# Layer 1 of a two-block transformer kernel in a pinned order with PSUM tiles, and 14 weight buffers in MLP 0

## The chip, the cores and the metric

The kernel runs on 1 core of one Trainium2 chip, in one launch. The metric is the device time of that core in microseconds (us); lower is better.

## The reference, cut to what matters

Sequence length 256, width 1024, float32 throughout. Two blocks follow each other; the change touches the first one, whose second layer is a gated linear recurrence.

```python
def mixer_c(h, w_in, conv_w, conv_b, w_r, b_r, w_i, b_i, lam, w_out):
    u = h @ w_in                                    # 1024 -> 2048
    gate, xr = jnp.split(u, 2, axis=-1)
    xr = causal_depthwise_conv(xr, conv_w) + conv_b # width 4
    y = rg_lru(xr, w_r, b_r, w_i, b_i, lam) * jax.nn.gelu(gate)
    return y @ w_out

def rg_lru(x, w_r, b_r, w_i, b_i, lam):             # 8 heads of 128
    r = sigmoid(einsum("bshi,hij->bshj", xb, w_r) + b_r)
    i = sigmoid(einsum("bshi,hij->bshj", xb, w_i) + b_i)
    log_a = -8.0 * r * softplus(-lam)
    a = exp(log_a); mult = sqrt(-expm1(2.0 * log_a))
    return scan(h_t = a_t * h_(t-1) + mult * i * x)

def first_block(x, ...):
    for layer in range(2):
        h = rmsnorm(x, mix_norm[layer])
        x = x + (mixer_ab(h, ...) if layer == 0 else mixer_c(h, ...))
        h = rmsnorm(x, mlp_norm[layer])
        x = x + square(relu(h @ w_up[layer])) @ w_down[layer]   # 1024 -> 4096 -> 1024
    return rmsnorm(x, final_norm)
```

The second block (latent attention and neighbourhood attention, with a modulation computed from a conditioning vector) follows; its arithmetic is untouched.

## The kernel before, in words

Activations lie transposed: 8 tiles of 128 channels by 256 positions. Every matrix product is made in three passes on TensorE (PE), high half times high half (L360), high times low (L361), low times high (L362), each a 128x128 weight against 256 columns. The host lays all weights out in the order of use, as 231 **units** of 128x1024 numbers (512 KB). One unit is 8 weights, so 24 products.

A unit takes this way: a DMA from SP's queue into one of RAW = 4 raw buffers (L300), a copy that makes the high half, on ACT (L307) or DVE (L309), and a subtraction that makes the low half, on DVE or POOL (L310). Which engines do it is set by `POLICY` for each name: "a" or "v" for the high half, "v" or "g" (POOL) for the low one. In layer 1 the names are `xr` (8 units, recurrence input), `ri` (2 units, the gates of four heads each), `cg` (8 units, the gelu branch) and `wo1` (8 units, the output product). `ready()` prepares the next unit of the plan; `unit(name)` takes one from the queue `self.q` and first prepares until `ahead` more stand behind it. Each `unit()` also runs one step of a background list, which in MLP 0 holds the modulation: 12 DMAs of 1 MB (`mw`) and 40 reductions on DVE (L883).

Prepared units lie in slots: RING = 6 (`wh`, `wl`) and, while the pool `wx` is open, EXTRA = 4 more (`wxh`, `wxl`). In MLP 0 `ahead` goes from 2 to FAR = 6 at pair 10 of 16:

```python
for p in range(16):
    if l == 0 and p == 10:
        self.ahead = FAR
    up(p)
```

The end of MLP 0 is `proj_tail` (L820 to L861): the last four units of `down` for all columns, in four column blocks, and after each block the residual sum on DVE (L835, L836), the high half of the next layer's input on ACT (L841, `xsh`), its low half on DVE (L847, `xsl`), a square on ACT (L855) and the running sum of squares on DVE (L857, `s`); at the end POOL folds the two halves of that sum (L861).

Layer 1 begins with `gfirst`, which interleaves the first two pairs of `xr` units by their depth: 6 of 8 steps of pair 0, 3 of pair 1, the rest of pair 0, the rest of pair 1. The norm comes in between: the column sums on PE (L424, `csum`), the variance on DVE (L430), its power -1/2 on POOL (L435, `rc`), and after both pairs the spread of it over the partitions on PE (L442) and ACT (L448, `R`). Each pair is then scaled by `R` (L1034), convolved over four taps by ACT (L1038) and DVE (L1042) into the SBUF tile `xc`, split into `xch` (ACT, L399) and `xcl` (DVE, L407) for each head, multiplied by the head's gate weights, passed through tanh (L1018, L1019, L1022) and exp (L1023), squared on DVE (L1026, L1027), rooted on ACT (L1057), scanned on DVE (L1064), multiplied by the gelu of the gate branch (L1048, L1050, L1066) and split for the output product (`xr`, `ysl`). Pair 3 of `xr` stands behind the first gate unit (RI0 = 6).

The order on each engine is set by a scheduler from priorities in program order and from dependences; `issue_after` adds a single edge.

Of the kernel before, what the change touches and what calls it, by code (L numbers as in the profile page):

```python
# [27 lines left out]
EXTRA = 4  # L28
FAR = 6
# [15 lines left out]
POLICY.update(val=("av", "ag", "av", "ag"), gate=("av", "av", "av", "ag"), xr=("av", "ag"), ri=("vg",), cg=("vg",))  # L45
# [24 lines left out]
def weight_plan(I):  # L70
# [48 lines left out]
    ri(1)  # L119
    for j in range(8):  # L120
        inn("cg", w, j * 128)
# [127 lines left out]
class Kern:  # L249
    def __init__(self, tc, aps, names, ctx):  # L250
        self.tc, self.nc, self.a, self.names, self.ctx = tc, tc.nc, aps, names, ctx
        self.n = 0
        self.u = 0
        self.raw = None
        self.bg = []
        self.q = []
        self.cnt = {}
        self.ahead = 2
        self.wx = None
        self.slot = 0  # L260

# [50 lines left out]
    def ready(self):  # L312
# [26 lines left out]
        self.q.append((name, (wh, wl)))  # L339

# [35 lines left out]
    def gfirst(self, name, x, mid=None):  # L376

        ps, ws = [self.ps(), self.ps()], [[], []]
        for a, k0, k1 in ((0, 0, GA), (1, 0, GB), (0, GA, 8), (1, GB, 8)):
# [7 lines left out]
            if k1 == 8 and mid:  # L387
                mid()
                mid = None
# [38 lines left out]
    def meaneps(self, ps, n, nt=2, tag="var"):  # L428
        v = self.t(self.cp, [128, nt], tag, bufs=2)
        self.nc.vector.tensor_scalar(v, ps, 1.0 / n, EPS, op0=ALU.mult, op1=ALU.add)  # L430
        return v
# [84 lines left out]
    def new_h(self, tag="xs"):  # L516
        return (self.t(self.cp, [128, 8, T], tag + "h", F32R), self.t(self.cp, [128, 8, T], tag + "l", F32R))
# [300 lines left out]
    def proj_tail(self, acc, name, ins, gname, g0, xs, R2=None, mp=None, sums=(), after=None):  # L818
# [4 lines left out]
        with self.tc.issue_after(after.ins) if after else nullcontext():  # L823
            ws = [self.unit(name) for _ in ins]
        n = len(ins)
        late = []
        for b in range(4):
# [17 lines left out]
            if xs is not None:  # L845
                for k in ks:
                    V.scalar_tensor_tensor(xs[1][:, k], x[:, k], g[k % 2], xs[0][:, k].bitcast(F32),  # L847
                                           op0=ALU.mult, op1=ALU.subtract)
            for i, (st, scaled) in enumerate(sums):
# [4 lines left out]
                else:  # L854
                    S.activation(q, xb, AF.Square)  # L855
# [4 lines left out]
        for st, _ in sums:  # L860
            G.tensor_tensor(st[:, 0], st[:, 0], st[:, 1], op=ALU.add)  # L861

    def mod_setup(self, mp):
# [4 lines left out]
        tv = self.t(mp, [128, 2048], "tv")  # L868
# [70 lines left out]
    def mlp(self, mp, l):  # L939
# [22 lines left out]
        for p in range(16):  # L962
            if l == 0 and p == 10:
                self.ahead = FAR
# [22 lines left out]
    def layer1(self, lp):  # L987
# [8 lines left out]
        xc = self.t(lp, [128, 8, T], "xc")  # L996
# [4 lines left out]
        parts = [self.s1[:, 0]]  # L1001
        rc = []
        self.ahead = 2
        pss = self.gfirst("xr", xs, lambda: rc.append(self.rsq(self.meaneps(self.csum(parts), D))))
        R = self.spread(lp, rc[0], "R")

        def ri(u):
            w = self.unit("ri")
            hs = range(4 * u, 4 * u + 4)
            for h in hs:  # L1010
                xch = self.t(lp, [128, T], "xch", F32R, bufs=2)
                xcl = self.t(lp, [128, T], "xcl", F32R, bufs=2)
                self.split(xc[:, h], xch, xcl)
                ps = self.ps("acc")
                for i in range(2):
                    c = slice(((h % 4) * 2 + i) * 128, ((h % 4) * 2 + i + 1) * 128)
                    self.mm3(ps[:, i * T:(i + 1) * T], (w[0][:, c], w[1][:, c]), (xch, xcl), True, True)
                S.activation(r[:, h], ps[:, :T], AF.Tanh, bias=hb[:, h:h + 1], scale=0.5)  # L1018
                S.activation(ig[:, h], ps[:, T:], AF.Tanh, bias=hb[:, 8 + h:9 + h], scale=0.5)  # L1019
                V.scalar_tensor_tensor(ig[:, h], ig[:, h], 1.0, xc[:, h], op0=ALU.add, op1=ALU.mult)  # L1020
            for h in hs:
                S.activation(th[:, h], r[:, h], AF.Tanh, scale=sp[:, h:h + 1], bias=sp[:, h:h + 1])  # L1022
                last = S.activation(r[:, h], r[:, h], AF.Exp, scale=nsp[:, h:h + 1], bias=nsp[:, h:h + 1])  # L1023
                if h % 2:
                    sl = slice(h - 1, h + 1)
                    V.tensor_tensor(xc[:, sl], r[:, sl], r[:, sl], op=ALU.mult)  # L1026
                    V.scalar_tensor_tensor(th[:, sl], xc[:, sl], 1.0, th[:, sl], op0=ALU.add, op1=ALU.mult)  # L1027
            return last

        for p in range(4):  # L1030
            if 2 * p == RI0:
                ri(0)
            ps = pss[p] if p < 2 else self.gpair(("xr", "xr"), xs)
            V.tensor_tensor(xr[:, 2 * p:2 * p + 2, 3:], self.pair(ps), self.b2(R), op=ALU.mult)  # L1034
            ca = self.pair(self.ps("acc"))
# [3 lines left out]
            for i in range(3):  # L1039
                for h in range(2):  # L1040
                    j = 2 * p + h
                    V.scalar_tensor_tensor(xc[:, j] if i == 2 else ca[:, h], xr[:, j, i:i + T],  # L1042
                                           self.p("ccw", j * 4 + i), ca[:, h], op0=ALU.mult, op1=ALU.add)

        def gate_pair(p):
            ps = self.gpair(("cg", "cg"), xs)
            xg = gl[:, 2 * p:2 * p + 2]
            V.tensor_tensor(xg, self.pair(ps), self.b2(R), op=ALU.mult)  # L1048
            with self.tc.issue_after(sq.ins):
                S.activation(xg, xg, AF.Gelu_apprx_tanh)  # L1050
# [483 lines left out]
```

## Time and profile before

| what | us |
| --- | --- |
| median of 3 runs | 832.42 (828.91 to 835.37) |
| the profiled execution, its own time | 829.35 |
| its span | 827.5 |
| PE busy | 790.3 (96% of the span) |
| DVE, ACT, POOL busy | 589.2, 457.4, 220.6 |
| layer 1, first to last product | 93.30 (291.92 to 385.22) |
| granted clock of PE, mean | 0.987 |

The profiled execution lies 3.07 under the median of the runs; 1.85 us of it lie around the span. All times of the trace are counted from the start of the span. The granted clock is a share of full speed: 1.00 stands for 2.4 GHz and 0.50 for 1.2 GHz, the two levels that exist.

### The profile page before, as it was taken

The numbers are of one execution on the slowest core, as the hardware profiler recorded it, in microseconds if no ns is written. First come the engines' busy times: TensorE is split into PE (matmuls) and PEld (weight loads), VectorE is DVE, ScalarE is ACT, GpSimd is POOL, SyncE is SP. The second block draws the span as 40 slices with busy tenths as digits, with TensorE's granted clock in tenths as the row PEclk, the third lists the DMA queues.
The fourth block names the chain that finished last, engine by engine and source line by source line (L and its number), as shares of the span: only waits on it lengthen the run. The fifth ranks groups of instructions, "written<-read, shape, count | busy, mean of one in ns | idle before, by whom it ended". The sixth has DMA issues, their size and how long they took to land.

```text
span 827.5 us, 16152 instructions
## 1 busy us (share of the span) xinstructions
PE 790.3 (96%) x6476; PEld 757.8 (92%) x6476; DVE 589.2 (71%) x956; ACT 457.4 (55%) x722; POOL 220.6 (27%) x160
## 2 busy tenths in 40 slices
PE   6999899999999978798999999999999999999996
PEld 6997799999999978698999999999989988889996
DVE  6899659999997698898638445557634877566743
ACT  5578546544446625576636444545626587765433
POOL 4886634110111465500441101111000022220001
PEclk9999999999999999799999999999999999999998
DMA  7864357878878744318646566665234532554621
GB/s 237 305 204 128 102 179 240 336 269 301 289 275 280 250 120 136 112 49 303 222 126 202 185 183 201 191 194 177 85 126 142 165 104 101 179 166 166 204 78 51
DMA packets 41259, 152.32 MB, mean 184 GB/s; under 512 B 4576, under 2 KB 5088, under 8 KB 39008
## 3 DMA queue, kind: packets, MB, share of 16 engines
q1 hardware_dynamic: 40752, 149.19, 55.4%
q10 hardware_dynamic: 432, 2.10, 0.6%
q8 instruction: 51, 0.84, 0.4%
q14 instruction: 24, 0.20, 0.1%
HBM read 149.17 MB, written 2.10 MB: 183 GB/s over the span
## 4 chain that ended last, share of the span: by engine, by line
PE 74%; DVE 11%; ACT 5%; DMA 3%; issue 3%; POOL 2%; SPq 0%; POOLq 0%; DVEq 0%; ACTq 0%
PE mm L360 13%; PE mm L361 13%; PE mm L362 12%; PE acc L361 10%; PE acc L360 9%; PE acc L362 9%; DMA raw<-in_wst 3%; PE acc L1320 2%; PE acc L1348 2%; PE mm L1357 2%; DVE wl L310 2%; ACT wh L307 1%; DVE ysl L407 1%; POOL wl L310 1%; PE mm L442 1%
## 5 line engine op out<-in xcount | busy, mean ns | idle before, releaser
L307 ACT ACTIVATE wh<-raw 128x1024 fp32r<-128x1024 f32 (+1 forms) x198 | 207.1, 1049 | 185.6 <-PE mm L361 77.3
L310 DVE TENSOR_TENSOR wl<-raw,wh 128x1024 fp32r<-128x1024 f32 (+1 forms) x167 | 208.8, 1257 | 109.5 <-ACT wh L307 109.4
L361 PE MATMUL mm<-xsl,wh 128*128 128x256 f32 x824 | 229.7, 279 | 1.5 <-DVE xsl L847 1.5
L360 PE MATMUL mm<-xsh,wh 128*128 128x256 f32 x824 | 231.0, 280 | 0.0
L362 PE MATMUL mm<-xsh,wl 128*128 128x256 f32 x824 | 229.6, 279 | 0.0
L360 PEld LDWEIGHTS mm<-xsh,wh 128*128 128x128 f32 x824 | 156.0, 189 | 3.7 <-issue 3.3
L361 PEld LDWEIGHTS mm<-xsl,wh 128*128 128x128 f32 x824 | 156.0, 189 | 2.6 <-DVE xsl L847 2.1
L362 PEld LDWEIGHTS mm<-xsh,wl 128*128 128x128 f32 x824 | 155.6, 189 | 0.0
L957 POOL TENSOR_TENSOR ma<-mr 128x512 f32<-128x512 f32 x32 | 49.7, 1554 | 233.7 <-ACT mr L955 233.7
L361 PE MATMUL acc<-mal,wh 128*128 128x256 f32 x384 | 106.6, 278 | 0.7 <-DVE mal L407 0.7
L360 PE MATMUL acc<-mah,wh 128*128 128x256 f32 x384 | 106.7, 278 | 0.0
L362 PE MATMUL acc<-mah,wl 128*128 128x256 f32 x384 | 106.3, 277 | 0.0
L310 POOL TENSOR_TENSOR wl<-raw,wh 128x1024 fp32r<-128x1024 f32 x36 | 87.9, 2463 | 27.9 <-ACT wh L307 27.2
L361 PEld LDWEIGHTS acc<-mal,wh 128*128 128x128 f32 x384 | 72.4, 188 | 1.3 <-DVE mal L407 1.3
L362 PEld LDWEIGHTS acc<-mah,wl 128*128 128x128 f32 x384 | 72.1, 188 | 0.0
L360 PEld LDWEIGHTS acc<-mah,wh 128*128 128x128 f32 x384 | 72.1, 188 | 0.0
L307 ACT ACTIVATE wxh<-raw 128x1024 fp32r<-128x1024 f32 x35 | 36.6, 1056 | 34.7 <-DMA raw<-in_wst 27.0
L883 DVE CUSTOM_DVE_ANT_0 mdump<-mw,cv 128x1024 f32<-128x1024 f32 x40 | 51.0, 1274 | 3.4 <-DMA mw<-in_modw 3.1
L310 DVE TENSOR_TENSOR wxl<-raw,wxh 128x1024 fp32r<-128x1024 f32 x34 | 43.7, 1305 | 9.4 <-ACT wxh L307 9.4
L361 PE MATMUL mm<-xsl,wxh 128*128 128x256 f32 x168 | 47.5, 283 | 1.9 <-DVE xsl L847 1.9
L360 PE MATMUL mm<-xsh,wxh 128*128 128x256 f32 x168 | 47.6, 284 | 0.2 <-ACT xsh L841 0.2
L362 PE MATMUL mm<-xsh,wxl 128*128 128x256 f32 x168 | 47.2, 281 | 0.0
(374 smaller groups left out, 1765.1 us busy)
## 6 DMA issues: line engine op xcount, KB each, us to landing
raw<-in_wst SPq DMA_DIRECT2D x240, 512.0 KB, 4.1
mw<-in_modw SPq DMA_DIRECT2D x12, 1024.0 KB, 7.5
nb<-in_nab SPq DMA_DIRECT2D x16, 256.0 KB, 3.6
ab<-in_alibi ACTq DMA_DIRECT2D x1, 1536.0 KB, 7.8
x<-in_xT SPq DMA_DIRECT2D x4, 256.0 KB, 5.2
cv<-in_cvec SPq DMA_DIRECT2D x1, 1024.0 KB, 4.7
cx<-in_cT SPq DMA_DIRECT2D x1, 1024.0 KB, 6.5
xd<-x SPq DMA_DIRECT2D x1, 1024.0 KB, 4.4
```

The costliest lines, as they stand in the source:

```text
L307: nc.scalar.activation(wh, r, AF.Copy)
L310: (nc.vector if lo == "v" else nc.gpsimd).tensor_tensor(wl, r, wh.bitcast(F32), op=ALU.subtract)
L360: mm(out, w[0], x[0], start=start, stop=False, skip_group_check=True)
L361: mm(out, w[0], x[1], start=False, stop=False, skip_group_check=True)
L362: return mm(out, w[1], x[0], start=False, stop=stop, skip_group_check=True)
L407: self.nc.vector.tensor_tensor(l, src, h.bitcast(F32), op=ALU.subtract)
L442: self.lasts = self.nc.tensor.matmul(ps[:, j * 128:(j + 1) * 128], rc[:, j:j + 1].to_broadcast([128, 128]), self.ident, start=True, stop=True)
L883: V.tensor_tensor_reduce(d, w, cv[:, s * 1024:(s + 1) * 1024], 0.5, 0.0, op0=ALU.mult, op1=ALU.add, accum_out=self.mod[:, s * 24 + i:s * 2 ...
L957: G.tensor_tensor(a, r, r, op=ALU.mult)
L1320: PE.matmul(sc[i], Q[tag, h][a][:, qs], K[tag, h][b], start=a + b == 0, stop=a == 1)
L1348: PE.transpose(pt[:, i * 128:(i + 1) * 128], P[:, i * 128:(i + 1) * 128], self.ident)
L1357: PE.matmul(o[64 * hh:64 * hh + 64, :T], vt[:, i, h * 64:h * 64 + 64], PTs[tag, h][:, i], start=i == 0, stop=i == 3, skip_group_check=True)
```

## The change

It has five parts.

- *Buffers.* EXTRA is 6, so there are 12 slots, and from pair 9 of MLP 0 two more are lent by a pair of tiles (`hch`, `hcl`, 2112 columns wide) that the second block uses later. `ahead` becomes min(2p - 14, 13) from pair 9: 4, 6, 8, 10, 12, 13, 13. In layer 1 `ahead` is 0 and the program calls `more(n)`, which prepares n units at that place. `proj_tail` takes its units with a falling `ahead` and prepares a few after each column block.
- *Engines.* `xr` and `ri` units have their high halves on ACT and their low ones on DVE, four of the `cg` and four of the `wo1` units have them on POOL; the second `ri` unit stands behind `cg` unit 1 in the plan.
- *The norm.* `gfirst` with a list runs 36 products of pair 0, then the column sums (over two parts, so POOL's fold goes), then 24 products, then the spread, then the other 36 of pair 1.
- *PSUM.* The convolution stays in PSUM (`ca` in the tiles `acc`) and is read there by the splits and the gates; the gates' products lie in tiles `mm`; the squares of the decay go from DVE to ACT and into PSUM.
- *The order.* `inorder` chains all instructions of PE and of ACT in layer 1 in program order, with edges that wait for nothing. The roots and scans are done by halves, the gelus by two pairs, so that ACT loads a function table five times in layer 1 where it loaded one twice.

```diff
-EXTRA = 4
-FAR = 6
+EXTRA = 6
+FAR = 2
-POLICY.update(..., xr=("av", "ag"), ri=("vg",), cg=("vg",))
+POLICY.update(..., xr=("av",), ri=("av",), cg=("av", "av", "av", "av", "ag", "ag", "ag", "ag"))
-POLICY["wo1"] = ("ag",) * 2 + ("av",) * 6
+POLICY["wo1"] = ("ag",) * 4 + ("av",) * 4
-    ri(1)
     for j in range(8):
+        if j == 2:
+            ri(1)
         inn("cg", w, j * 128)
+        else:
+            c = 16 + 1024 * (self.slot - RING - EXTRA)
+            wh, wl = [h[:, c:c + 1024] for h in self.hs]
+    def more(self, n):
+        for _ in range(n):
+            self.ready()
+        if mid:
+            plan = ((0, 0, 6), (0, 6, 8), (1, 0, 2), (1, 2, 8))
...
-            ws = [self.unit(name) for _ in ins]
+            ws = [self.unit(name, len(ins) - 1 - i) for i in range(len(ins))]
+            self.more(max(0, min(1 + b, 3) - len(self.q)))
-        for st, _ in sums:
+        for st, _ in sums if mp and xs is None else ():
             G.tensor_tensor(st[:, 0], st[:, 0], st[:, 1], op=ALU.add)
-            if l == 0 and p == 10:
-                self.ahead = FAR
+            if l == 0 and p >= 9:
+                if p == 9:
+                    self.hs = [self.t(self.cp, [128, 2112], f"hc{c}", F32R) for c in "hl"]
+                self.ahead = min(2 * p - 14, 13)
...
+        with self.inorder(PE.engine):
+            pss = self.gfirst("xr", xs, (norm, None, scale))
+        with self.tc.issue_after(self.lastv.ins), self.tc.issue_after(self.lastsq.ins):
+            self.more(4)
+        with self.inorder(*PIN):
+            conv(0, pss[0])
+            conv(1, pss[1])
+            self.more(3)
+            self.hs, self.slot = None, self.slot % (RING + EXTRA)
+            p2 = self.gpair(("xr", "xr"), xs)
+            heads(0)
+            heads(1)
+            gates(0, ri(0))
+            conv(2, p2)
+            tanhs(0)
+            p3 = self.gpair(("xr", "xr"), xs)
+            conv(3, p3)
+            decay(0)
+            decay(1)
+            self.more(1)
+            cg(0)
+            heads(2)
+            heads(3)
+            gates(1, ri(1))
+            self.more(1)
+            root(0)
+            cg(1)
+            gelu(0)
+            gelu(1)
+            done(0)
+            self.more(1)
+            tanhs(1)
+            cg(2)
+            done(1)
+            decay(2)
+            decay(3)
+            self.more(1)
+            cg(3)
+            root(1)
+            gelu(2)
+            gelu(3)
+            self.more(2)
+            for k in range(4):
+                if k >= 2:
+                    done(k)
+                wrow(k)
+                self.more(1 if k == 0 else 2)
+            wrow(4)
```

Here `heads` splits a pair's convolution, `gates` runs the sigmoids of four heads, `tanhs` and `decay` make the recurrence's factors, `root` the square roots, their products and the scans of four heads, `cg` one pair of the gate branch, `done` multiplies and splits one pair of channels, and `wrow` is one unit of the output product. The loop over `wrow` is written shorter here than in the code.

The first place is DVE at the border of MLP 0 and layer 1. The names: L835/L836 (after: L866/L867) are the residual sum, `xsl` the input's low half, `s` the sum of squares, `wh` and `wl` halves of weight units, `var` the variance. Before:

```order
L836 TENSOR_TENSOR x_75<-x_75,acc_1440 128x512
L857 TENSOR_TENSOR s_5_76<-s_5_76,mm_3687 128x512
L310 TENSOR_TENSOR wxl_3911<-raw_3908,wxh_3910 128x1024
L847 SCALAR_TENSOR_TENSOR xsl_3568<-x_75,par_70,xsh_3567 128x256 x2
L857 TENSOR_TENSOR s_5_76<-s_5_76,mm_3720 128x512
L309 CAST wh_4025<-raw_4023 128x1024
L309 CAST wh_4055<-raw_4053 128x1024
L430 TENSOR_SCALAR var_3818<-mm_3815 128x2
L309 CAST wh_4095<-raw_4093 128x1024
L309 CAST wh_4173<-raw_4171 128x1024
L309 CAST wh_4203<-raw_4201 128x1024
```

And after:

```order
L878 SCALAR_TENSOR_TENSOR xsl_3602<-x_75,par_70,xsh_3601 128x256
L867 TENSOR_TENSOR x_75<-x_75,acc_1446 128x512
L889 TENSOR_TENSOR s_5_76<-s_5_76,mm_3697 128x512
L878 SCALAR_TENSOR_TENSOR xsl_3602<-x_75,par_70,xsh_3601 128x256 x2
L889 TENSOR_TENSOR s_5_76<-s_5_76,mm_3730 128x512
L458 TENSOR_SCALAR var_3798<-mm_3793 128x2
L326 TENSOR_TENSOR wl_3870<-raw_3867,wh_3869 128x1024
L326 TENSOR_TENSOR wl_3876<-raw_3873,wh_3875 128x1024
L326 TENSOR_TENSOR wxl_3882<-raw_3879,wxh_3881 128x1024
L326 TENSOR_TENSOR wxl_3888<-raw_3885,wxh_3887 128x1024
```

Three weight operations stood between the last residual sum (L836) and the variance (L430); now none does, and four low halves of weights follow the variance.

The second place is ACT behind the gates of the last heads. `th`, `r` and `ig` are the recurrence's factors, `gl` the gelu branch, `xr` the high half of the output product's input, `wh` the high half of a weight unit. Before:

```order
L1023 ACTIVATE r_3743<-r_3743,sm_1846 128x256
L1022 ACTIVATE th_3744<-r_3743,sm_1846 128x256 x2
L1023 ACTIVATE r_3743<-r_3743,sm_1846 128x256 x2
L1057 ACT_TABLE_LOAD
L1057 ACTIVATE th_3744<-th_3744 128x1024 x2
L1050 ACT_TABLE_LOAD
L1050 ACTIVATE gl_3746<-gl_3746 128x512 x3
L307 ACTIVATE wh_4480<-raw_4478 128x1024
L399 ACTIVATE xr_4167<-xc_3742 128x512
L307 ACTIVATE wh_4510<-raw_4508 128x1024
```

And after:

```order
L323 ACTIVATE wh_4231<-raw_4229 128x1024
L1103 ACT_TABLE_LOAD
L1103 ACTIVATE th_3752<-th_3752 128x1024
L1115 ACT_TABLE_LOAD
L1115 ACTIVATE gl_3754<-gl_3754 128x512 x2
L427 ACTIVATE xr_4292<-th_3752 128x512
L323 ACTIVATE wh_4300<-raw_4298 128x1024
L1091 ACTIVATE th_3752<-r_3751,sm_1846 128x256 x4
L427 ACTIVATE xr_4292<-th_3752 128x512
L1095 ACT_TABLE_LOAD
L1095 ACTIVATE r_3751<-r_3751,sm_1846 128x256 x2
L1098 ACTIVATE acc_4363<-r_3751 128x512
```

The root is taken by halves, gelu and the splits of the first channels come ahead of the second half's tanh and exp, and the weight copies stand at fixed places among them; a second round of square, root and gelu follows before the next copies.

The third place is SP's queue in MLP 0, where `raw` is a weight unit and `mw` a transfer of the modulation. Before:

```order
L880 DMA mw_2915<-in_modw 128x2048
L300 DMA raw_2651<-in_wst 128x1024
L300 DMA raw_2683<-in_wst 128x1024
L300 DMA raw_2716<-in_wst 128x1024
L880 DMA mw_3054<-in_modw 128x2048
L300 DMA raw_2722<-in_wst 128x1024
L300 DMA raw_2728<-in_wst 128x1024
L300 DMA raw_2734<-in_wst 128x1024
L880 DMA mw_3231<-in_modw 128x2048
```

And after:

```order
L912 DMA mw_2927<-in_modw 128x2048
L316 DMA raw_2730<-in_wst 128x1024
L316 DMA raw_2734<-in_wst 128x1024
L316 DMA raw_2740<-in_wst 128x1024
L316 DMA raw_2774<-in_wst 128x1024
L316 DMA raw_2814<-in_wst 128x1024
L316 DMA raw_2846<-in_wst 128x1024
L316 DMA raw_2879<-in_wst 128x1024
L912 DMA mw_3074<-in_modw 128x2048
```

Between two neighbouring transfers of the modulation stood three units; between these two now stand seven.

## Rows read from the trace of the kernel before

**Rows 1.** The page, part 1: busy time, share of the span, instructions.
```profile
PE 790.3 (96%) x6476; PEld 757.8 (92%) x6476; DVE 589.2 (71%) x956; ACT 457.4 (55%) x722; POOL 220.6 (27%) x160
```

**Rows 2.** The windows view, six stretches: busy us of each engine (instructions), granted clock, DMA share, GB/s.
```profile
204.50:253.60 49.10, 49.10 (x436) 49.10 (x434) 44.57 (x58) 22.07 (x26) 5.97 (x4) 1.00 0.82 285
253.60:283.90 30.30, 30.11 (x266) 29.92 (x265) 19.35 (x18) 20.02 (x24) 11.68 (x7) 1.00 0.83 274
291.92:385.22 93.30, 80.05 (x634) 77.41 (x633) 80.92 (x107) 48.92 (x84) 35.63 (x16) 0.93 0.43 134
310.00:314.00 4.00, 4.00 (x24) 4.00 (x23) 1.78 (x3) 2.58 (x5) 4.00 (x3) 0.57 0.49 142
340.70:348.00 7.30, 6.41 (x28) 6.12 (x29) 5.78 (x10) 4.12 (x10) 2.21 (x1) 0.50 0.48 148
385.22:392.00 6.78, 4.70 (x31) 3.70 (x30) 6.78 (x12) 5.90 (x9) 0.00 (x0) 1.00 0.90 304
```

**Rows 3.** The waits of PE, 291.92 to 392 us: total, times, longest, us.
```profile
PE acc L361 <- DVE xcl L407: 7.7, 4, 5.1
PE mm L361 <- DVE xsl L847: 3.4, 4, 1.5
PE mm L442 <- POOL rc L435: 3.0, 1, 3.0
```

**Rows 4.** The timeline of PE, first products of layer 1: start, us, operation.
```profile
291.92 0.28 PE L360 MATMUL mm<-xsh,wh 128*128 128x256 f32 x1
...
294.64 0.28 PE L360 MATMUL mm<-xsh,wh 128*128 128x256 f32 x1
```

**Rows 5.** The timeline of PE around the longest wait, idle before in brackets.
```profile
335.36 0.28 PE L361 MATMUL mm<-xsl,wh 128*128 128x256 f32 x1
...
340.74 0.58 PE L361 MATMUL acc<-xcl,wh 128*128 128x256 f32 x1 [5.10 <-DVE xcl L407]
```

**Rows 6.** Groups by line and shape, 291.92 to 372 us: count, busy, mean ns.
```profile
L310 POOL TENSOR_TENSOR wl<-raw,wh 128x1024 fp32r<-128x1024 f32 x8 | 20.8, 2626 | 0.0
...
L307 ACT ACTIVATE wh<-raw 128x1024 fp32r<-128x1024 f32 x7 | 7.2, 1049 | 0.0
...
L1042 DVE SCALAR_TENSOR_TENSOR acc<-xr,par,acc 128x256 f32<-128x256 f32 x16 | 7.2, 478 | 1.0 <-ACT acc L1038 1.0
...
L310 DVE TENSOR_TENSOR wl<-raw,wh 128x1024 fp32r<-128x1024 f32 x4 | 4.9, 1220 | 1.5 <-ACT wh L307 1.5
...
L1034 DVE TENSOR_TENSOR xr<-mm,R 128x512 f32<-128x512 f32 x4 | 2.6, 682 | 1.3 <-ACT R L448 1.3
...
L1050 ACT ACTIVATE gl<-gl 128x512 f32<-128x512 f32 x4 | 2.3, 625 | 0.0
```

**Rows 7.** The timeline of ACT at the square roots of layer 1.
```profile
350.04 0.47 ACT L1018 ACTIVATE r<-acc,hb 128x256 f32<-128x256 f32 x1
350.39 0.48 ACT L1019 ACTIVATE ig<-acc,hb 128x256 f32<-128x256 f32 x1
...
352.23 1.09 ACT L1023 ACTIVATE r<-r,sm 128x256 f32<-128x256 f32 x2
353.34 1.28 ACT L1057 ACT_TABLE_LOAD   x1
354.63 2.01 ACT L1057 ACTIVATE th<-th 128x1024 f32<-128x1024 f32 x2
```

**Rows 8.** The timeline of DVE, 338 to 341 us.
```profile
338.12 0.48 DVE L1042 SCALAR_TENSOR_TENSOR acc<-xr,par,acc 128x256 f32<-128x256 f32 x1
338.51 2.17 DVE L407 TENSOR_TENSOR xcl<-xc,xch 128x256 fp32r<-128x256 f32 x1
```

**Rows 9.** The timeline of POOL over the same time.
```profile
337.61 5.29 POOL L310 TENSOR_TENSOR wl<-raw,wh 128x1024 fp32r<-128x1024 f32 x2
```

**Rows 10.** The page, part 6: queue, count, KB each, us to landing.
```profile
raw<-in_wst SPq DMA_DIRECT2D x240, 512.0 KB, 4.1
```

**Rows 11.** The timeline of DVE in MLP 0, one reduction of the modulation.
```profile
227.26 1.22 DVE L883 CUSTOM_DVE_ANT_0 mdump<-mw,cv 128x1024 f32<-128x1024 f32 x1 [1.74 <-DMA mw<-in_modw]
```

More of the change, by code (lines that the diff above doesn't have):

```diff
@@ L260, in __init__, with inorder @@
         self.slot = 0
+        self.hs = None
+    @contextmanager
+    def inorder(self, *engines):
+        traced = self.nc.cur_bb.bb.instructions
+        old = {id(i) for i in traced}
+        yield
+        last = {}
+        for i in traced:
+            if id(i) not in old and i.engine in engines:
+                if i.engine in last:
+                    self.tc.add_manual_dep(i, last[i.engine].name, mybir.DependencyInfo(
+                        mybir.DependencyClass.NoSync, mybir.DependencyReason.DATA), reason="issue_after")
+                last[i.engine] = i
     def pool(self, name, space=None):
@@ L1000, in layer1 @@
         gl = self.t(lp, [128, 8, T], "gl")
-        parts = [self.s1[:, 0]]
+        parts = [self.s1[:, 0], self.s1[:, 1]]
         rc = []
[L1003 to L1033, printed above, removed]
+        self.ahead = 0
+        PIN = (PE.engine, S.engine)
+        def norm():
+            rc.append(self.rsq(self.meaneps(self.csum(parts), D)))
+        def scale():
+            rc.append(self.spread(lp, rc[0], "R"))
+        with self.inorder(PE.engine):
+            pss = self.gfirst("xr", xs, (norm, None, scale))
+        R = rc[1]
+        with self.tc.issue_after(self.lastv.ins), self.tc.issue_after(self.lastsq.ins):
+            self.more(4)
@@ L1068, in layer1, with heads, ri @@
-        acc = [self.ps("acc") for _ in range(4)]
-        for k in range(5):
-            self.krow(acc, self.unit("wo1"), (ys[0][:, k], ys[1][:, k]), k == 0, False)
+        def heads(p):
+            for h in (2 * p, 2 * p + 1):
+                sp3[h] = (self.t(lp, [128, T], "xch", F32R, bufs=4), self.t(lp, [128, T], "xcl", F32R, bufs=4))
+                self.split(cas[p][:, h % 2], *sp3[h])
+        def ri(u):
+            w = self.unit("ri")
+            out = []
+            for h in range(4 * u, 4 * u + 4):
+                ps = self.ps()
+                for i in range(2):
+                    c = slice(((h % 4) * 2 + i) * 128, ((h % 4) * 2 + i + 1) * 128)
+                    self.mm3(ps[:, i * T:(i + 1) * T], (w[0][:, c], w[1][:, c]), sp3[h], True, True)
+                out.append(ps)
+            return out
@@ new lines, in gates, with tanhs @@
+        def gates(u, pr):
+            for h in range(4 * u, 4 * u + 4):
+                ps = pr[h % 4]
+                S.activation(r[:, h], ps[:, :T], AF.Tanh, bias=hb[:, h:h + 1], scale=0.5)
+                S.activation(ig[:, h], ps[:, T:], AF.Tanh, bias=hb[:, 8 + h:9 + h], scale=0.5)
+                V.scalar_tensor_tensor(ig[:, h], ig[:, h], 1.0, cas[h // 2][:, h % 2], op0=ALU.add, op1=ALU.mult)
+        def tanhs(u):
+            for h in range(4 * u, 4 * u + 4):
+                S.activation(th[:, h], r[:, h], AF.Tanh, scale=sp[:, h:h + 1], bias=sp[:, h:h + 1])
@@ new lines, in cg, with gelu, done, wrow @@
+        def cg(p):
+            ps = self.gpair(("cg", "cg"), xs)
+            V.tensor_tensor(gl[:, 2 * p:2 * p + 2], self.pair(ps), self.b2(R), op=ALU.mult)
+        def gelu(p):
+            S.activation(gl[:, 2 * p:2 * p + 2], gl[:, 2 * p:2 * p + 2], AF.Gelu_apprx_tanh)
+        def done(p):
+            hp = slice(2 * p, 2 * p + 2)
+            V.tensor_tensor(th[:, hp], th[:, hp], gl[:, hp], op=ALU.mult)
+            self.split(th[:, hp], ys[0][:, hp], ys[1][:, hp])
+        def wrow(k):
+            self.krow(acc, self.unit("wo1"), (ys[0][:, k], ys[1][:, k]), k == 0, False)
@@ L1071, in layer1 @@
+        self.ahead = 2
         xs = self.new_h()
```

85 lines of the change are left out of this document (47 added, 38 removed).

## The prediction

> **What bounds the kernel now.** I read the page first. TensorE works for 790.3 of 827.5 us [rows 1], so a change can gain only where PE waits, restarts, or runs below its clock; I looked for those stretches with the windows view, then asked the waits view who ends them, and went to the timelines for the sizes.
>
> MLP 0 gives nothing: PE is busy for 49.10 of 49.10 us and for 30.11 of 30.30 us at its tail [rows 2]. Layer 1 is the place. It lasts 93.30 us, 291.92 to 385.22 [rows 2], and works off 26 units. One unit is 24 products and takes 294.64 − 291.92 = 2.72 us [rows 4], so 26 units need 70.7 us and 22.6 us are lost. The waits view names 14.1 us of it: 7.7 for the low half of a gate head's input (`xcl`), 3.4 for the low half of layer 1's input (`xsl`), 3.0 for the norm's power on POOL (`rc`) [rows 3]. The longest wait, 5.10, is a gap of 5.38 us from one start to the next [rows 5], so a restart adds 0.2 to 0.3. The rest is clock: after the two long waits the granted clock falls to 0.57 and 0.50, that is to the level of 1.2 GHz, and 24 products take 4.00 us (1.3 lost) or 28 take 6.41 of busy time (3.2 lost) [rows 2]. The start of MLP 1 loses too: 31 products, worth 3.5 us, in 6.78 [rows 2].
>
> Why is `xcl` late? On DVE a low half with two SBUF inputs takes 2.17 us while POOL subtracts a weight's low half, and the tap with PSUM operands just ahead of it takes 0.48 [rows 8, 9]. One POOL low takes 2.63 [rows 6].
>
> **The change part by part**, in times of the profiled execution.
>
> *Start of layer 1.* No weight preparation is left between DVE's last residual operations and the variance, the sum over two parts drops POOL's fold, and POOL has no weight to subtract before `rc`. The first two pairs are 4 units, 10.9, with the sum and the transposed norm beside them at 0.9: 11.8, to 303.7. That removes the 3.0 of `rc` and about 2.5 of the `xsl` waits; the half clock after `rc` goes with them.
>
> *Pair 2 and gates 0.* Pair 2 is 2 units, 5.4, to 309.1. The heads need DVE's chain from the variance (296.9): 4 weight lows at 1.22, 3 scalings at 0.65, 12 taps at 0.45, one more low, 4 input lows at 0.43 = 15.0 [rows 6, 8], with 0.9 of small waits at 312.8. PE wants the fourth head at 309.1 + 2.0 = 311.1: a wait of 1.8, then 2.7 for the unit. The input low with one PSUM operand is in no row. It lies between 0.39 (the step of a tap) and 2.17 (the low with two SBUF inputs); I take 0.43, as the tap beside POOL's low stays short. At the upper end four of them add 7 us.
>
> *Pair 3, gate pair 0, gates 1.* 4 units, 10.9, to 324.5. On ACT, from the gates of the first half: 8 tanh at 0.35, two conv starts, four more tanh, two more starts, four exponentials at 0.55 [rows 7], two squares into PSUM, the weight copy of gate unit 6 at 1.05, then the head's high half, at 325.7. The squares stand in no row; the nearest operation of this size is the gelu's 0.63 [rows 6], bounds 0.35 to 1.05, too little to matter. Waits 1.7, unit 2.7.
>
> *Gate pairs 1 to 3.* 6 units, 16.3, to 345.3. Nothing here is late.
>
> *The output product.* It is 8 units, 21.8, but here the pinned order of ACT hurts. From the last gate (330.1) ACT runs, in this order: a weight copy 1.05, table 1.28, root 1.0, table 1.28, two gelus 1.25, a split 0.6, a weight copy 1.05, four tanh, a split, table 1.28, four exponentials and two squares; with about 1.9 of waits for DVE this is 16.7, to 346.8. Only then comes the copy for the output's second unit (347.9), and POOL subtracts for 2.4 more: 350.3 against PE at 348.0, a wait of 2.2. Then come table, root, table, two gelus (4.8, to 352.7) before the third unit's copy: 353.7, POOL at 356.1, a wait of 3.1. The raw buffer of the seventh unit comes free with that subtraction; its transfer lands 4.1 later [rows 10], its copy ends at 361.3, and the split of channel pair 2, queued behind it, leaves DVE at 363.1 against PE at 361.4: 1.6. Together 6.9. For the POOL low I took 2.4 to 2.6; were it hidden these waits would be near 0.
>
> Each table load was priced at 1.28 without anything around it: the exponential ends at 353.32, the load starts at 353.34 and the root at 354.63 [rows 7]. The Trainium skill ("ScalarE: Activation LUTs", What ACT_TABLE_LOAD costs) says that a switch also drains for about 1.38 us, 2.66 in all. The trace shows no such drain around this load; the rule's own result is a rival below.
>
> Sum of layer 1: 11.8 + 5.4 + 1.8 + 2.7 + 10.9 + 1.7 + 2.7 + 16.3 + 21.8 + 6.9 = 82.0 against 93.3, a gain of 11.3.
>
> *Around it.* MLP 1's start has more weights ready: of its 3.3 lost I count 1.5 back (bounds 0 and 3.3). Against this: half clock after the output's waits, 1.5 (1.3 to 3.2 from the two stretches above); restarts of some nine waits at about 0.2, 1.7; and MLP 0's end, 0.5. There DVE takes six more weight lows (7.3 us) and the transfers three more units. DVE idles for 4.5 + 10.9 us in the two last windows [rows 2], so there is room, and the transfers at 285 and 274 GB/s would have to reach about 301, as the 304 of a later window shows possible [rows 2]; PE has no slack there, so what doesn't fit is paid whole (0 to 6).
>
> Gain 11.3 + 1.5 − 1.5 − 1.7 − 0.5 = 9.1. The profiled execution took 829.35, of which 827.5 is span; it becomes 820.2. The median of the runs stands 3.1 above the profiled one, so the prediction is 823.3.
>
> **The rivals.** A measurement of this kernel can tell about 1% (8.3 us) from no change.
>
> *The output product doesn't wait (0.20).* If POOL's lows and ACT's chain come as early as PE needs them, 6.9 goes, with it the clock loss, but restarts stay: about 816.9. For it: POOL does only eight lows in layer 1 now. Against it: the copies stand behind the roots in a pinned order. Faster.
>
> *MLP 0 pays for the filling (0.14).* The reductions of the modulation stand in DVE's order before weight lows, and one waited 1.74 us for its transfer [rows 11]; the extra units sit ahead of those transfers in SP's queue, seven between two of them where three stood. Three or four such waits cannot be hidden, as PE has no gap there: 4 to 6 us, about 828.5. Against it: the 15.4 us of idle DVE. Within 1% (0.13), else slower (0.01).
>
> *Every table load costs a drain (0.03).* Five loads at 1.38 more on ACT's chain are 6.9 us at the output product: 830.2, within 1%. Against it rows 7. By the skill's rule named above this would be the forecast.
>
> *The clock stays low through the output product (0.11).* After each of its waits PE restarts cold, and the waits are 3 us apart or so. If the clock is granted at half from the second unit on, as from 340.7 to 348.0 [rows 2], 7 units of 24 products take twice 0.113 us each: 168 × 0.113 = 19.0 more. Slower products let the late weights catch up (4.3 of the waits go) and the 1.5 is counted already: +13.2, 836.5. It decides from about 9 us lost, that is once half clock covers four of these units. For it: both long waits of layer 1 were followed by such a stretch. Against it: the first one was over within 4 us, and these waits are half as long. Slower by over 1% in 0.06, within 1% in 0.05.
>
> **How the numbers follow.** The forecast holds 0.52, its own range 818 to 829; over 1% faster begins at 824.1, so that 0.32 of it is faster and 0.20 the same. With the rivals: faster 0.32 + 0.20 = 0.52; same 0.20 + 0.13 + 0.03 + 0.05 = 0.41; slower 0.07. The range from 812 to 833 leaves out the upper half of the clock rival and the case in which several bounds go well together; it holds an input low at its upper end (830.3).
>
> **What would show it.** In the profile after, PE's wait on `rc` should be gone and that on `xcl` short; the first four units of layer 1 should take under 12.5 us; ACT should show five table loads in layer 1; PE's waits in the output product should name POOL's `wl` on the second and third unit. PE should have no gap over 1 us in MLP 0. I am wrong if layer 1 takes over 88 us or under 78, if the granted clock is near 0.5 through the output product, or if MLP 0 is longer by over 2 us.

## The result and the profile after

The changed kernel took 821.38 us (median of 4 runs, 821.14 to 821.60), the kernel before beside it 832.89; the ratio is 0.9877 with a 95% interval of 0.9833 to 0.9920. The prediction was 823.3. A later series gave 823.46 (8 runs, 820.01 to 826.46), ratio 0.9908 (0.9876 to 0.9940). So the gain is 11.5 us in the first series and 9.4 in the second, against 9.1 forecast.

The windows view of the changed kernel: two stretches of MLP 0, all of layer 1, its output product, the half-clock stretch in that, and the first 6.78 us of MLP 1 (columns as in [rows 2]).

```profile
204.50:253.60 49.10, 49.10 (x436) 49.10 (x435) 46.09 (x59) 22.98 (x27) 5.76 (x4) 1.00 0.90 316
253.60:284.90 31.30, 30.46 (x269) 30.26 (x268) 25.44 (x28) 20.97 (x24) 6.31 (x4) 1.00 0.82 276
293.00:380.08 87.08, 78.56 (x638) 75.87 (x637) 64.00 (x99) 63.25 (x101) 21.61 (x10) 0.98 0.38 127
348.52:380.08 31.56, 25.31 (x194) 24.01 (x193) 24.76 (x26) 22.29 (x28) 7.55 (x3) 0.95 0.56 189
354.00:358.00 4.00, 3.74 (x21) 3.74 (x22) 3.83 (x7) 3.97 (x6) 0.58 (x2) 0.60 0.38 131
380.08:386.86 6.78, 6.23 (x52) 5.91 (x51) 6.70 (x11) 5.02 (x9) 0.00 (x0) 1.00 0.89 287
```

Layer 1 takes 87.08 us where it took 93.30, and MLP 1 does 52 products in its first 6.78 us where it did 31 [rows 2]. Layer 1 begins 1.1 later (293.00 instead of 291.92); only part of that arises in MLP 0, as told further below. The waits of PE in layer 1 answer to [rows 3]:

```profile
PE acc L385 <- POOL wl L326: 2.9, 2, 1.5
PE acc L384 <- DVE ysl L435: 2.5, 2, 1.6
PE mm L384 <- DVE xcl L435: 1.2, 2, 0.8
PE mm L383 <- ACT xch L427: 0.9, 1, 0.9
PE acc L383 <- DVE th L1099: 0.7, 1, 0.7
PE acc L383 <- ACT xr L427: 0.2, 1, 0.2
```

The wait on `rc` is gone, that on `xcl` fell from 7.7 to 1.2, and new waits in the output product (POOL's `wl`, `ysl`, `th`, `xr`) sum to 6.3 (the 7.4 of the expectations has the restarts in it). The longest is 1.6, and in this execution only one stretch at half clock follows, 12 products near 355 us, where before some 40 products ran at that rate in two stretches.

### The profile page after: what moved, and what is told of

Same layout as the page of the kernel before. It is cut to its first block, busy times and chain, and to the rows that moved or that the text cites. A ratio compares the mean times of both kernels' runs of the same rounds, so it can differ in the third digit from the quotient of the medians.

```text
span 819.4 us, 16154 instructions
## 1 busy us (share of the span) xinstructions
PE 787.9 (96%) x6480; PEld 756.0 (92%) x6480; DVE 576.4 (70%) x952; ACT 473.2 (58%) x739; POOL 199.0 (24%) x151
## 4 chain that ended last, share of the span: by engine, by line
PE 59%; issue 19%; DVE 8%; ACT 8%; POOL 4%; DMA 2%; SPq 0%; POOLq 0%; DVEq 0%; ACTq 0%
PE mm L383 10%; PE mm L384 10%; PE mm L385 10%; PE acc L384 7%; PE acc L383 7%; PE acc L385 7%; POOL ma L989 3%; PE acc L1423 2%; PE acc L1451 2%; PE mm L1460 2%; ACT wh L323 1%; DMA raw<-in_wst 1%; DVE wl L326 1%; PE mm L470 1%; DMA x<-in_xT 1%
## 5 line engine op out<-in xcount | busy, mean ns | idle before, releaser
L326 DVE TENSOR_TENSOR wl<-raw,wh 128x1024 fp32r<-128x1024 f32 (+1 forms) x159 | 197.6, 1250 | 100.1 <-ACT wh L323 98.3
L383 PE MATMUL mm<-xsh,wh 128*128 128x256 f32 x752 | 210.4, 280 | 0.0
L384 PE MATMUL mm<-xsl,wh 128*128 128x256 f32 x752 | 209.1, 278 | 0.0
L385 PE MATMUL mm<-xsh,wl 128*128 128x256 f32 x752 | 209.1, 278 | 0.0
L383 PEld LDWEIGHTS mm<-xsh,wh 128*128 128x128 f32 x752 | 141.7, 188 | 3.7 <-issue 3.3
L384 PEld LDWEIGHTS mm<-xsl,wh 128*128 128x128 f32 x752 | 141.7, 188 | 0.6 <-DVE xsl L878 0.2
L385 PEld LDWEIGHTS mm<-xsh,wl 128*128 128x128 f32 x752 | 141.3, 188 | 0.0
L326 POOL TENSOR_TENSOR wl<-raw,wh 128x1024 fp32r<-128x1024 f32 x31 | 74.2, 2414 | 43.8 <-ACT wh L323 43.8
L323 ACT ACTIVATE wxh<-raw 128x1024 fp32r<-128x1024 f32 x47 | 49.2, 1055 | 38.8 <-DMA raw<-in_wst 34.9
L326 DVE TENSOR_TENSOR wxl<-raw,wxh 128x1024 fp32r<-128x1024 f32 x44 | 56.6, 1299 | 8.0 <-ACT wxh L323 8.0
```

The source lines that it names most:

```text
L323: nc.scalar.activation(wh, r, AF.Copy)
L326: (nc.vector if lo == "v" else nc.gpsimd).tensor_tensor(wl, r, wh.bitcast(F32), op=ALU.subtract)
L383: mm(out, w[0], x[0], start=start, stop=False, skip_group_check=True)
L384: mm(out, w[0], x[1], start=False, stop=False, skip_group_check=True)
L385: return mm(out, w[1], x[0], start=False, stop=stop, skip_group_check=True)
```

## The experiments

Twelve runs were made, the last of them (e11) the changed kernel again. Times are medians, ratios those to the kernel before on the same chip, with 95% intervals. "Layer 1" is from its first product to the first of MLP 1, read in PE's timeline of the profiled execution. That is one execution, and not always a typical one: it lies 5.5 us above the median of its kernel in e8, 3.6 in e10 and 3.0 in e5, and 4.2 below it in e9. So waits and stretches are read from the traces, and gains from the medians.

**The filling alone (e1).** The kernel before with `EXTRA = 6`, the lent tiles, the growing `ahead` and the falling one in `proj_tail`; layer 1 in its old order. One of its lines, where the lent tiles are given back (the `lambda` is cut short):

```diff
+        self.hs, self.slot = None, self.slot % (RING + EXTRA)
         pss = self.gfirst("xr", xs, lambda: ...)
```

> The kernel before with the 14 buffers and their filling in MLP 0 (and the falling number of prepared units at its end), layer 1 as before. Theory (most of the gain is layer 1's order): MLP 0 gets 1 us longer, the wait on rc shrinks because fewer preparations stand at the start of layer 1, the waits on xcl stay; 829 to 832 us, a gain of 1 to 4. Rival (the deeper filling is the gain): 821 to 825, with layer 1 under 88 us.

833.06 us, ratio 1.0023 (0.9988 to 1.0058): no gain. But layer 1 took 87.02 us, as little as in the changed kernel; MLP 0 gave it all back, as layer 1 began at 299.46. The rival had layer 1 right and the time wrong; neither theory said that MLP 0 would pay so much. PE's waits, then DVE and POOL beside the longest:

```profile
PE mm L369 <- DVE xsl L858: 5.8, 4, 2.5
PE acc L369 <- DVE mal L415: 5.3, 1, 5.3
```

```profile
280.09 3.44 DVE L311 TENSOR_TENSOR wl<-raw,wh 128x1024 fp32r<-128x1024 f32 x1 [0.17 <-ACT wh L308]
284.46 2.81 DVE L415 TENSOR_TENSOR mal<-ma,mah 128x512 fp32r<-128x512 f32 x1 [0.93 <-POOL ma L969]
```

```profile
280.05 2.40 POOL L311 TENSOR_TENSOR wl<-raw,wh 128x1024 fp32r<-128x1024 f32 x1 [0.69 <-DVE wh L310]
282.39 2.04 POOL L969 TENSOR_TENSOR ma<-mr 128x512 f32<-128x512 f32 x1
284.39 2.33 POOL L311 TENSOR_TENSOR wl<-raw,wh 128x1024 fp32r<-128x1024 f32 x1
```

POOL's weight subtraction at 280.05 delays its own `ma`, and the next one, at 284.39, stretches DVE's `mal` to 2.81 us (0.69 in the changed kernel at 282.73). PE has no slack there: 5.3 us, and half clock after it.

**The filling with DVE lows (e9).** e1 with the low halves of `xr` and `ri` units on DVE; the high halves of the two `ri` units go from DVE to ACT with them.

```diff
-xr=("av", "ag"), ri=("vg",)
+xr=("av",), ri=("av",)
```

> The kernel with the filling alone, and besides it the low halves of xr and ri units on DVE, as the change has them; layer 1 in its old order. Theory (in the filling alone MLP 0 paid because POOL's weight subtractions delayed its own multiplications and stretched DVE's low halves): the wait of 5.3 us in MLP 0's last units falls under 1.5 and the waits on xsl at the start of layer 1 from 6.1 under 2; 824 to 829. Rival (the extra transfers or DVE's extra work set it): both waits stay over 4 us, 831 to 835.

828.15 us, ratio 0.9952 (0.9921 to 0.9984). The wait of 5.3 in MLP 0 fell to nothing (layer 1 begins at 291.19), so the theory holds there. The waits on `xsl` stayed, against the theory, as POOL still subtracts at that place (the `cg` units, whose policy was left) and DVE's low halves fall beside it. The waits, then one such place, two low halves of 128x256 in 5.11 us:

```profile
PE mm L369 <- DVE xsl L858: 6.3, 4, 2.4
PE acc L369 <- DVE xcl L415: 1.8, 1, 1.8
```

```profile
292.41 5.11 DVE L858 SCALAR_TENSOR_TENSOR xsl<-x,par,xsh 128x256 fp32r<-128x256 f32 x2
```

```profile
292.03 2.70 POOL L311 TENSOR_TENSOR wl<-raw,wh 128x1024 fp32r<-128x1024 f32 x1 [11.88 <-DVE wh L310]
294.70 2.54 POOL L311 TENSOR_TENSOR wxl<-raw,wxh 128x1024 fp32r<-128x1024 f32 x1
```

Layer 1 took 87.67 us. So the filling and one policy edit, in the old order and with no pin, bring layer 1 down nearly as far as the changed kernel's order does. The largest lack against it that the traces show is MLP 1's start (30 products in its first 6.78 us, 52 in the changed kernel; 20.02 us for its first 144 products instead of 17.87). That is 2.2 of the 4.7 us between the medians of e9 and e11; where the rest lies is not shown, and the two intervals just overlap. Whether the waits on `xsl` would go with the `cg` lows on DVE too was not tried.

**The order alone (e2).** The changed kernel with `EXTRA = 4` and `FAR = 6` from pair 10, no lent tiles.

```diff
-                self.ahead = min(2 * p - 14, 13)
+                self.ahead = FAR
```

> The changed kernel with the old filling: 10 buffers, 6 units ahead from pair 10. Theory: layer 1's order works as well with four units less in the queue; MLP 0 loses its extra 1 us and layer 1 takes 87 to 90 us; 820 to 825. Rival (the deeper filling is the gain): PE waits for weights in layer 1, 828 to 833.

840.53 us, ratio 1.0121 (1.0080 to 1.0163): slower. Layer 1 takes 103.92. The theory fell. The queue is shorter: 98 low halves are done when layer 1 begins, 103 in the changed kernel. The copies, which stand at fixed places in ACT's order, come too late one after the other, and three groups of waits for weights are each followed by half clock (the longest waits, then three windows):

```profile
PE mm L383 <- ACT wh L323: 5.3, 2, 2.9
PE mm L384 <- DVE xcl L435: 4.4, 3, 2.5
PE acc L383 <- ACT wxh L323: 3.1, 1, 3.1
```

```profile
338.00:342.00 4.00, 3.54 (x16) 3.24 (x17) 2.86 (x5) 3.97 (x4) 0.00 (x0) 0.50 0.45 127
353.00:357.00 4.00, 3.94 (x18) 3.94 (x19) 2.45 (x1) 3.94 (x7) 2.38 (x2) 0.50 0.37 131
373.00:377.00 4.00, 3.74 (x17) 3.74 (x18) 0.00 (x0) 0.62 (x1) 4.00 (x3) 0.50 0.56 150
```

**ACT unpinned (e3) and half pinned (e8).** `PIN = (PE.engine,)`, and the pin of ACT ending after the gates of the second half.

> The changed kernel with only PE pinned in layer 1, ACT left to the scheduler. Theory (the pinned ACT order delays the weight copies of the output product): PE's waits there fall from 7.4 to under 4 us; 817 to 820. Rival (without the pin ACT puts weight copies or table loads ahead of the heads' splits): waits at the gate units grow, more table loads, 823 to 828.

> The changed kernel with ACT pinned only up to the gates of the second half, PE pinned throughout. Theory (the pin helps at the gate units and hurts at the output product): the waits at the gate units stay at 3 us as in the changed kernel, those of the output product go as with ACT unpinned; 814 to 818. Rival (what ACT gains there is lost again at the start of MLP 1, where the unpinned kernel waited 3 us): 819 to 822.

823.00 us, ratio 0.9909 (0.9881 to 0.9937), and 822.47, ratio 0.9899 (0.9863 to 0.9935): no different from the changed kernel. In e3 the waits of the output product vanish, as the theory had it, and those at the gate units grow from 2.1 to 5.8, as the rival had it; ACT loads nine tables in layer 1 instead of five. Layer 1 takes 85.68 us, 1.4 less than in the changed kernel, but the first 144 products of MLP 1 take 20.00 instead of 17.87. In e8 the waits at the gate units grow to 6.9, though the pin was left there: what stands behind the gates in the program is no longer held there and comes between the splits of the heads. At the first half it is weight copies (the two rows below: a copy that waited 2.2 us for its transfer, and the last split behind it), at the second copies and also table loads, of which e8 has six. The start of MLP 1, which the rival of e8 named, has no part in it: its first 144 products take 16.96 us. So the pin moves the waits from one place to the other.

```profile
319.57 1.06 ACT L323 ACTIVATE wh<-raw 128x1024 fp32r<-128x1024 f32 x1 [2.19 <-DMA raw<-in_wst]
320.53 0.37 ACT L427 ACTIVATE xch<-acc 128x256 fp32r<-128x256 f32 x1
```

All of e3's waits in layer 1:

```profile
PE mm L384 <- DVE xcl L435: 3.4, 2, 2.2
PE mm L383 <- ACT xch L427: 2.5, 2, 1.5
```

**The norm late (e4).** The old plan of `gfirst`, with `(None, None, norm, scale)`.

> The changed kernel with the norm where it stood before: the old interleaving of the first two pairs, column sums after pair 0, the spread after both pairs. Theory (the early norm feeds DVE's chain to the first gate unit): the wait before the gates of heads 0 to 3 grows from 2 to about 5 us, and the clock falls after it; 824 to 827. Rival (with POOL and DVE free of weights at that place the norm's place costs nothing): 821 to 822.

826.76 us, ratio 0.9942 (0.9914 to 0.9969). Layer 1 takes 91.20, 4.1 more; in the first gate unit PE waits 4.0 us instead of 0.8, and half clock follows (21 products). MLP 1's first 144 products then take 1.2 less. The theory holds.

**The convolution in SBUF (e5).**

```diff
-V.scalar_tensor_tensor(ca[:, h], xr[:, j, i:i + T],
+V.scalar_tensor_tensor(xc[:, j % 4] if i == 2 else ca[:, h], xr[:, j, i:i + T],
```

> The changed kernel with the last tap of the convolution written to SBUF again (a tile of four heads, used twice), so that the splits and gates read SBUF; all else as changed. Theory (the low half of a head's input is short because one of its operands lies in PSUM, whatever POOL does): the lows that fall beside a POOL subtraction take over 1.5 us instead of 0.4, PE waits 3 to 5 us more at the gate units; 824 to 828. Rival (POOL has only few subtractions there, the place doesn't matter): 821 to 822.

The splits and the gates then read `xc`. 829.22 us, ratio 0.9956 (0.9934 to 0.9978). Layer 1 takes 93.01, 5.9 more, the wait on `xcl` 5.2 instead of 1.2. In e5 POOL subtracts from 313.28 to 318.25, and two of the low halves fall beside it:

```profile
314.49 1.54 DVE L435 TENSOR_TENSOR xcl<-xc,xch 128x256 fp32r<-128x256 f32 x1
316.34 2.18 DVE L435 TENSOR_TENSOR xcl<-xc,xch 128x256 fp32r<-128x256 f32 x1
```

In the changed kernel POOL subtracts from 309.91 to 315.03, and the same operation with one operand in PSUM is not touched:

```profile
311.08 0.42 DVE L435 TENSOR_TENSOR xcl<-acc,xch 128x256 fp32r<-128x256 f32 x1 [0.24 <-ACT xch L427]
312.80 0.42 DVE L435 TENSOR_TENSOR xcl<-acc,xch 128x256 fp32r<-128x256 f32 x1
```

It takes both: where POOL is idle, two SBUF operands cost nothing. In e1 POOL does nothing between 336.87 and 344.58, and two of these operations take 0.74 us together:

```profile
337.08 0.74 DVE L415 TENSOR_TENSOR xcl<-xc,xch 128x256 fp32r<-128x256 f32 x2
```

All eight of e1 take 0.41 or 0.42 each, none beside a subtraction of POOL. PE waits 1.8 us for `xcl` in all there, in the old order and without PSUM.

**Lows on DVE (e6).** `cg` and `wo1` all `("av",)`.

> The changed kernel with the low halves of all units of the gate branch and of the output product on DVE instead of eight on POOL. Theory (POOL's 2.4 us at the end of ACT's chain sets the waits on the output's second and third unit): each of these waits falls by about 1.2, but the eight subtractions cost DVE 9.6 us; 819 to 822. Rival (DVE becomes the bound in layer 1): 823 to 827.

823.72 us, ratio 0.9883 (0.9852 to 0.9914): no different from the changed kernel. POOL's waits became DVE's (2.4 us on `wl`, and 1.7 on a weight copy that is new), and `xcl`, now behind more of DVE's lows, waits 4.3 us. The time lies in the rival's range, at its lower end. The waits of the output product fell by 1.4, those at the gate units grew by 3.4.

**Two table loads (e7), and with earlier copies (e10).** e7 puts the second half's tanh, exponentials and squares ahead of both roots. e10 also moves copies ahead of the first splits and holds the second half's scans back:

```diff
+            tanhs(1)
+            decay(2)
+            decay(3)
+            sqrt(0)
+            sqrt(1)
             root(0)
             cg(1)
...
             gelu(1)
+            self.more(2)
             done(0)
```

> The changed kernel with the second half's tanh, exponentials and squares ahead of the first square root, both roots together and then the gelus: two table loads in layer 1 instead of five. Theory (ACT's pinned chain sets the waits of the output product): ACT saves 3.9 us there and PE's waits in the output product fall from 7.4 to under 4; 816 to 819. Rival (the first output rows come later because the first root stands behind the second half): 821 to 825.

> The changed kernel with the second half's tanh, exponentials and squares ahead of both roots (two table loads), but the roots' products and scans of the second half on DVE only after the first two pairs of the output's input are done, and the weight copies of the output's first two units in ACT's gap ahead of these. Theory (what is left to gain in layer 1 is the output product's 7.4 us of waits and the half clock after them): waits there under 2 us, 812 to 817. Rival (POOL's subtractions then fall beside DVE's products and scans and stretch them, so the second half comes late): waits of 3 to 6 us in one place and half clock after it, 820 to 825.

e7: 827.29 us, ratio 0.9919 (0.9890 to 0.9949). e10: 826.80, ratio 0.9935 (0.9910 to 0.9959). Neither gained over the changed kernel, as the rivals had it, but both times lie above the rivals' ranges. In e7 the waits of the output product fell from 6.3 to 4.3, nearly as the theory had it, but they are two that stand together, and half clock follows (21 products):

```profile
PE acc L383 <- ACT wh L323: 2.4, 1, 2.4
PE acc L385 <- POOL wl L326: 1.9, 1, 1.9
```

Its layer 1 is 1.5 us shorter than the changed kernel's (85.62), the first 144 products of MLP 1 take 1.1 more. In e10 ACT is in time, but POOL subtracts from 351.69 to 362.23 without a break and DVE's split falls into it:

```profile
354.44 5.55 DVE L435 TENSOR_TENSOR ysl<-th,xr 128x512 fp32r<-128x512 f32 x2
```

```profile
351.69 10.54 POOL L326 TENSOR_TENSOR wl<-raw,wh 128x1024 fp32r<-128x1024 f32 x3 [9.53 <-ACT wh L323]
```

**Both (e12).** e10 with `POLICY["wo1"] = ("av",)`.

> The kernel with two table loads and earlier weight copies, and the low halves of all eight units of the output product on DVE, so that POOL is idle in that stretch. Theory (it is POOL's subtraction that stretches DVE's low halves of the output's input, from 1.3 to 5.6 us for two): the wait of 2.8 us on the first of them falls to 1.5 to 2.2, as two weight lows now stand ahead of it on DVE, the later waits stay under 1 each; 818 to 822. Rival (DVE is full there): waits of over 4 us in the output product, 823 to 827.

816.85 us (6 runs, 814.87 to 819.73), ratio 0.9823 (0.9782 to 0.9864), below the forecast and below all 12 runs of the changed kernel, though on another chip than e10 and e11. Layer 1 takes 82.49, in e10 87.54, and the first 144 products of MLP 1 take 16.32 instead of 19.68. The same split, with POOL idle, and PE's waits:

```profile
349.51 2.35 DVE L326 TENSOR_TENSOR wl<-raw,wh 128x1024 fp32r<-128x1024 f32 x2
351.78 1.28 DVE L435 TENSOR_TENSOR ysl<-th,xr 128x512 fp32r<-128x512 f32 x2
```

```profile
PE acc L384 <- DVE ysl L435: 2.6, 2, 1.9
PE mm L383 <- ACT xch L427: 1.3, 1, 1.3
PE mm L384 <- DVE xcl L435: 1.2, 2, 0.7
```

These four lows on DVE without the new order were not tried (e6 moved the `cg` ones too), so that the new order is needed for this gain is not shown.

**The changed kernel again (e11).**

> The changed kernel once more, beside the two others on the same chip. Both theories: 820 to 823.5, with the waits of its first trace within 0.5 us each; where PE's pace between the waits changes, the time moves by up to 3 us without any wait moving.

823.46 us, as told above. The waits are not as steady as forecast: that of 1.57 on `ysl` is absent, one of 0.6 on a copy is new, and after the last of those on POOL's lows, 1.9, 26 products run at half clock instead of 12.

## Why the prediction was right

The sum held and its parts less so. Layer 1 was to take 82.0 with 1.5 of half clock and 1.7 of restarts, 85.2 in all; it took 87.08. MLP 1's start gave back 0.5 more than was counted, and later parts 1.0 that were not counted, which is luck. In the profiled executions the gain is 8.2 us, in the medians 11.5 and 9.4; the 9.1 lies between.

*Start of layer 1 and pair 2.* Forecast 11.8 + 5.4 = 17.2, measured 18.46 (293.00 to 311.46); the first four units took 12.80 of it, over the 12.5 named as a sign. The waits are gone; the rest is the column sums and the spread with their restarts (1.7 instead of 0.9) and a slower pace of PE from about 302 us on (below). The reason given was only half of it: the wait on `rc` is gone with the filling alone (e1) as well as with the order alone (e2), so either is enough. One reading was wrong: of the 3.4 us on `xsl` [rows 3] only 1.5 lie in layer 1, the other 1.9 in MLP 1, so there were no 2.5 to remove here; the sum does not use them. The early norm itself is worth 4.1 in layer 1 (e4).

*Gate units.* Forecast 1.8 + 2.7 and 1.7 + 2.7, measured 4.65 and, with the wait of 1.06 ahead of it, 4.79. The working for the first, DVE's chain, adds up to 15.2 and not 15.0. The low half at 0.42 was the right end of the range, and e5 shows why: a PSUM operand keeps it out of POOL's way. The Trainium skill ("SBUF — State Buffer", Who interferes with whom) says that a DVE instruction with two SBUF inputs contends with a POOL instruction that reads SBUF, and one with at most one SBUF input, outside its two-port modes, does not; the rows of e5 and of the changed kernel agree.

*The gate branch between.* Pair 3 and gate pair 0: forecast 10.9, measured 11.30 without a wait, at the slower pace. Gate pairs 1 to 3: forecast 16.3, measured 16.32 (332.20 to 348.52).

*Output product.* Forecast 21.8 + 6.9, with 1.5 of half clock; measured 31.56. The waits came from the places named, in other sizes: 1.47 and 1.45 on POOL's lows (forecast 2.2 and 3.1), 1.57 on pair 2 behind the late transfer (forecast 1.6), and 0.67, 0.15 and 0.94 that were not foreseen, of which the first is the release of an accumulator that still held a square. The sum, 6.3 against 6.9, was nearly right by luck: parts that cancel. For the first of them ACT's chain was added up too long: the terms named come to 16.2 and not 16.7, which would have given 1.7 instead of 2.2. That the pinned chain on ACT sets these waits is shown by e3, where they vanish with the pin; that the time would stay the same without the pin was not foreseen.

*Table loads.* Five, at 1.28 each, each begun within 0.02 of the operation before and followed within 0.02 by the next; the first of them:

```profile
333.59 1.12 ACT L323 ACTIVATE wh<-raw 128x1024 fp32r<-128x1024 f32 x1
334.72 1.28 ACT L1103 ACT_TABLE_LOAD   x1
336.02 1.06 ACT L1103 ACTIVATE th<-th 128x1024 f32<-128x1024 f32 x1
```

The drain of 1.38 us that the Trainium skill ("ScalarE: Activation LUTs", What ACT_TABLE_LOAD costs) adds to each does not occur here, so that rival falls.

*Around it.* MLP 1's first 144 products take 17.87 us instead of 19.86: 2.0 back (forecast 1.5). MLP 0's last 216 products, where the filling weighs, take 25.60 instead of 24.95: 0.65 paid (forecast 0.5), with a wait of 0.84 on `mal`. In the experiments whose MLP 0 is that of the changed kernel they take 24.5 to 25.5, and 28.2 in e10, where `mal` waits 1.35, so this price is not steady. The other 0.4 by which layer 1 begins later stands ahead of that. The span falls by 8.1: 6.2 in layer 1, 2.0 in MLP 1, less 1.1, and 1.0 in later parts that the change does not touch.

*The rivals.* Waits in the output product that don't bind: they did, 6.3 us. (By its own terms, 6.9 and 1.5 less, that rival stood at 814.9 and not at 816.9; both are on the same side.) MLP 0 paying for the filling: hardly in the changed kernel, though the modulation waited 2.6 us on DVE, but e1 shows a price beyond the rival's, 7.7 us in those 216 products, and by POOL's subtractions, not by the modulation's transfers. The clock low through the output product: 12 products in this execution, 26 in e11, not 168.

What the prediction missed is the tie between the parts. It added the order's gain to the filling's cost; in fact the order without the filling loses 1.2% (e2), the filling without the DVE lows gains nothing (e1), and filling and lows together make up about half of the whole (e9, 4.7 us where e11 on the same chip gained 9.4). In layer 1 the new order reaches no more than the filling does in the old one (87.08 against 87.02), so the account that layer 1's order removes the waits is right for this kernel and not the only way to it.

## What to carry to other kernels

When a large change moves little or much, run its parts alone: here one part alone is slower than before, and the sum is faster. A pinned order needs a queue deep enough for its fixed places. Where DVE and POOL work at once, look which operations have two SBUF inputs and keep POOL's long subtractions out of their way: moving four of them is the whole edit between e10 and e12, 0.9935 against 0.9823 of the time before.

## What the runs showed of the hardware

PE has two paces with the granted clock at 1.00. The same 48 us of the second block's end, before and after, with no wait in either:

```profile
757.34:805.34 48.00, 48.00 (x411) 48.00 (x410) 31.36 (x38) 21.61 (x25) 0.00 (x0) 1.00 0.47 161
```

```profile
750.71:798.71 48.00, 48.00 (x425) 48.00 (x424) 31.09 (x38) 21.41 (x25) 0.00 (x0) 1.00 0.48 160
```

411 products against 425. In PE's timeline 15 products take 1.76 us there before (786.88 to 788.64) and 1.70 after (779.74 to 781.44), that is 0.117 and 0.113 each. Some stretches of the slower pace lie at the same place of the program in all 14 profiled executions, others do not: the second block's end has it in all but the changed kernel's first execution and e12's. An estimate of their cost, from the blocks of 16 products whose steps average over 0.1155 us without a gap, is 5.6 us in the profiled execution before, 6.8 in the one after, and 4.3 to 9.5 in the experiments. The stretch shown here is worth 14 products, 1.6 us, more than the 1.0 by which the untouched parts differ. What sets the pace was not tried.

The pace is not the whole of the spread between executions of one kernel. By that estimate the changed kernel lost as much to it in e11 as in its first execution (6.6 and 6.8 us), and yet layer 1 began at 297.43 instead of 293.00. All of that arises in the first 744 products, long before the filling: 115.02 us instead of 109.62. In e11 the clock is granted at half for 13.7 us there, in three pieces, the first at 63 us where PE has just waited 1.75 us on DVE; in the first execution for 3.4 us, in one. One stretch of it, in e11 and then in the first execution:

```profile
40.00:75.00 35.00, 33.19 (x235) 28.70 (x234) 29.90 (x104) 25.05 (x65) 28.31 (x12) 0.95 0.61 182
```

```profile
40.00:75.00 35.00, 35.00 (x254) 30.76 (x254) 32.51 (x111) 26.17 (x66) 28.30 (x13) 1.00 0.65 195
```

The first 744 products end at 109.6 to 115.0 us in the 14 profiled executions. So where layer 1 begins tells of a change in MLP 0 only after what came earlier is taken off.
